# Decoder step on one core: k's projections issued before q's, part of each mLSTM head's preparation issued during q's projections, and 23 warm-up matmuls for 11

## The chip, the cores and the metric

One Trainium2 chip, one of its cores. The metric is the device time of one execution in microseconds (us); a single core runs the whole program.

## The reference, cut to what matters

One layer of a decoder for 1024 prompt tokens and 32 sample tokens (8 sequences of 4), width 1024. Each token is normalised and multiplied by `w_in`; the columns give the gMLP branch (u, v), the mLSTM branch (q, k, v, o and two gates per head) and two merge gates.

```python
qk = silu(causal_conv(qk_pad, conv_w, conv_b, T))      # q and k: 4-tap convolution over time
q, k = heads(qk[..., :W]), heads(qk[..., W:]) * 256 ** -0.5     # 4 heads of 256
...
# per head and chunk of tokens, C, n, m carried along:
s   = exp(dmat - m_t) * einsum('td,sd->ts', q, k)      # dmat: masked log decays
num = w_inter * einsum('vd,td->tv', C, q) + einsum('ts,sv->tv', s, v)
C   = decay * C + einsum('s,sv,sd->vd', w_in, v, k)
```

The rest (spatial gating, the two projections, `w_out`, a SwiGLU FFN and the norms) is the same in both kernels and is not touched by the change.

## The kernel before, in words

Every product in f32 is split: an operand becomes a rounded part (hi, fp32r) and a remainder (lo), and three matmuls stand for one. The input is kept transposed in `hT` (8 pairs of hi and lo, 128 x 1056).

A projection of 128 columns is one `TJob`: for each of 8 k-steps, 9 matmuls of 352 columns (hi and lo of the input for three column chunks, then the weight's remainder), then `evac`. `prep` of the next job splits its weight tile before the job at hand is run: ScalarE rounds `raw` to `wh` (L154) and VectorE subtracts for `wl` (L155). `wh` and `wl` have two buffers each, and the accumulator `acc` has two. Weights come by DMA on SP's queue into three `raw` buffers.

The order before is, for each head h: two TJobs for q, two for k, then a `Start` that puts the generator `mlstm(h)` into the queue `fill`, then 3 to 6 TJobs for the merge gates, two for o, and for later heads an `AJob` for v. After each k-step of a TJob `tick()` advances the first generator in `fill` to its next `yield`; so the mLSTM work of a head is spread through the projections that follow its k. A k-step is 9 matmuls.

`conv_evac` (q and k) copies `acc` out on ScalarE (L428 to L438), adds three taps on VectorE (L440, L442), applies Silu on ScalarE (L446), and writes the last raw rows through SP (L448).

`mlstm(h, q, k, so)` begins with the decay rows: `E` and `wb`, two of the 34 slots of the pool `S`, are filled by four DMAs from `nm_d` and `wi_d` (L578, L580), which `gates()` wrote in the first two projections of head 0. VectorE adds the mask to `E` (L588, L589), and ScalarE takes nine exponentials (L591, L592). After four more ticks comes `s1(0)`: 32 small transposes of k for token chunks 0 to 3 (`kt_part(0, n)`, L605), 8 of the 32 for chunks 4 to 7 (`kt_part(1, 0)`), the scores' two matmuls into the bank `s_ps`, `E = s_ps * E` on VectorE (L628), the scaled k (`kw`, L632, L633) and the split v (`vsp`). `s1(1)` to `s1(3)` have 8 transposes each. `s2(j)` has the state update's matmuls into two banks `u_ps`, `s3(j)` the output's into `n_ps`. The loop is

```python
        for _ in range(4):
            yield
        s1(0)
        yield
        for j in range(8):
            if j < 7:
                s1(j + 1)
                yield
            sq = s2(j)
            yield
            s3(j, *sq)
            yield
```

`s_ps`, `u_ps`, `n_ps` and other small results share the PSUM pool `pm` with two buffers; a new one waits until an older one was read. Except for the first stretch, where ScalarE, VectorE and SP have the written order, the Tile scheduler sets each engine's order; each engine then executes its own queue in that order.

At the start, 11 matmuls of zeros (`NWARM`, tile `wz`) run before the first data are there, and then `VStart`: for each 128 tokens the products of `hT` with two heads' v columns (`acc_v`), which need `avh` and `avl` (L206, L207) and the split input `hh`, `hl` (L382, L383).

Of the kernel before, what the change touches and what calls it, by code (L numbers as in the profile page):

```python
# [9 lines left out]
F32 = mybir.dt.float32  # L10
# [4 lines left out]
P = 128  # L15
D = 1024
TP = 1024
TS = 32
T = TP + TS
KT = D // P  # L20
H = 4
DH = 256
# [4 lines left out]
NF = DFF // P  # L27
EPS = 1e-6
NEG = -3.0e38
NWARM = 11  # L30
NCST = 4
FCH = ((0, 512), (512, 256), (768, 288))
REDO = (6, 7)
# [6 lines left out]
def hybrid_step_kernel(  # L40
# [9 lines left out]
    PE, V, A, G, SP = nc.tensor, nc.vector, nc.scalar, nc.gpsimd, nc.sync  # L50
# [4 lines left out]
    mp = ctx.enter_context(tc.tile_pool(name="mp", bufs=2))  # L55
# [4 lines left out]
    def S(name, dt=F32):  # L60
        return sp.tile([P, SLOT_W], dt, tag="s", name=name)

    def bank(name):
        return pm.tile([P, 512], F32, tag="sm", name=name)

    def f(ap):
        return ap.bitcast(F32)
# [48 lines left out]
    def mm(out, l, r, start, stop):  # L116
        PE.matmul(out, l, r, start=start, stop=stop)  # L117
# [160 lines left out]
    def add(job):  # L278
        jobs.append(job)
        for i, (src, j) in enumerate(job.parts):  # L280
            parts.append((src, job, i))
        job_end.append(len(parts))
# [30 lines left out]
    hT = [(S(f"hh{k}", F32R), S(f"hl{k}", F32R)) for k in range(KT)]  # L313
# [87 lines left out]
    vtiles = {}  # L401
# [17 lines left out]
    def conv_evac(kind, h, dt, dst):  # L419
        ct = 8 * kind + 2 * h + dt  # L420

        def ev(acc):
            raw = S("raw_qk")
            rs = raw[:, 1027:1083].rearrange("p (b s) -> p b s", s=7)
            G.memset(raw[:, 0:3], 0.0)
            G.tensor_copy(rs[:, :, 0:3],
                          scT[:, 24 * ct:24 * (ct + 1)].rearrange("p (b r) -> p b r", r=3))
            A.activation(raw[:, 3:707].rearrange("p (a c) -> p a c", c=CW), acc[:, 0:2, :CW], AF.Copy)  # L428
            A.activation(raw[:, 707:1027], acc[:, 2, 0:320], AF.Copy)
            A.activation(rs[:, :, 3:7], acc[:, 2, 320:352].rearrange("p (b t) -> p b t", t=LT), AF.Copy)  # L430
            c = S("qk")
            cs = c[:, TP:T].rearrange("p (b t) -> p b t", t=LT)

            def w(j):
                return cvw[:, 16 * j + ct:16 * j + ct + 1]
            A.activation(c[:, 0:704].rearrange("p (a c) -> p a c", c=CW), acc[:, 0:2, :CW], AF.Identity,
                         scale=w(3), bias=w(4))
            A.activation(c[:, 704:T], acc[:, 2, :CW], AF.Identity, scale=w(3), bias=w(4))  # L438
            for j in range(3):
                V.scalar_tensor_tensor(c[:, :TP], raw[:, j:j + TP], w(j), c[:, :TP],  # L440
                                       op0=ALU.mult, op1=ALU.add)
                V.scalar_tensor_tensor(cs, rs[:, :, j:j + 4], w(j), cs, op0=ALU.mult, op1=ALU.add)  # L442
            co = mp.tile([P, 27], F32, tag="co", name="co")
            G.tensor_copy(co[:, 0:3], raw[:, 1024:1027])
            G.tensor_copy(co[:, 3:27].rearrange("p (b r) -> p b r", r=3), rs[:, :, 4:7])
            A.activation(c[:, :T], c[:, :T], AF.Silu)  # L446
            dst[dt] = c
            SP.dma_start(conv_out[ct], co)  # L448
        return ev
# [118 lines left out]
    def colv(i, j, h, n=P):  # L568
        return cols[:n, i, 4 * j + h:4 * j + h + 1]

    def mlstm(h, q, k, so):
        E, wb = S("E"), S("wb")
        vs = vtiles.pop(h)

        def vt(j):
            return vs[j // 3][:, j % 3]
        for dst, src in ((E, nm_d), (wb, wi_d)):
            SP.dma_start(dst[:, :TP].rearrange("p (j t) -> p j t", t=P),  # L578
                         src[0:32].rearrange("(j h) t -> h j t", h=H)[h:h + 1].to_broadcast([P, 8, P]))
            SP.dma_start(dst[:, TP:T], src[32 + h:33 + h, 0:TS].to_broadcast([P, TS]))  # L580
        cst = {}

        def load_c(b):
            c = mp.tile([P, 2, DH], F32, tag="cst", bufs=NCST, name="cst")
            SP.dma_start(c, state_C[0, b, h].rearrange("(v p) d -> p v d", p=P))
            cst[b] = c
        E3 = E[:, :TP].rearrange("p (j t) -> p j t", t=P)
        V.tensor_tensor(E3, E3, maskneg.unsqueeze(1).to_broadcast([P, 8, P]), op=ALU.add)  # L588
        V.tensor_tensor(E[:TS, TP:T], E[:TS, TP:T], masks_s, op=ALU.add)  # L589
# [1 line left out]
            A.activation(E3[:, j], E3[:, j], AF.Exp, bias=colv(0, j, h))  # L591
        A.activation(E[:TS, TP:T], E[:TS, TP:T], AF.Exp, bias=colv(0, 8, h, TS))  # L592
        yield
        qk = {}
        Cx = [None, None, None]

        kts, vsp = {}, []

        def kt_part(g, n):
            if n == 0:  # L600
                kts[g] = S("kt")[:, :D].rearrange("p (j a c) -> p j a c", a=2, c=P)
            for i in range(8 * n, 8 * n + 8):
                dt, a, b = i // 16, i // 4 % 4, i % 4
                x = k[dt][32 * a:32 * a + 32, 512 * g:512 * (g + 1)].rearrange("p (j t) -> p j t", t=P)
                V.transpose(out=kts[g][32 * b:32 * b + 32, :, dt, 32 * a:32 * a + 32],  # L605
                            in_=x[:, :, 32 * b:32 * b + 32])

        def split(hi, lo, x, eng=V):
            A.activation(hi, x, AF.Copy)
# [7 lines left out]
        def s1(j):  # L617
            js = slice(P * j, P * (j + 1))
            if j == 0:
                for n in range(4):  # L620
                    kt_part(0, n)
            if j < 4:
                kt_part(1, j)
            b = bank("s_ps")
            for dt in range(2):
                mm(b[:, 0:P], k[dt][:, js], q[dt][:, js], dt == 0, dt == 1)
            sT = mp.tile([P, 2, P], F32R, tag="sT", name="sT")
            V.scalar_tensor_tensor(E3[:, j], b[:, 0:P], 0.0625, E3[:, j], op0=ALU.mult, op1=ALU.mult)  # L628
            split(sT[:, 0], sT[:, 1], E3[:, j])
            kt = kts[j // 4][:, j % 4].rearrange("p a c -> p (a c)")  # L630
            kw = mp.tile([P, 2, DH], F32R, tag="cst", bufs=NCST, name="kw")
            A.activation(kw[:, 0], kt, AF.Copy, scale=colv(1, j, h))  # L632
            V.scalar_tensor_tensor(kw[:, 1], kt, colv(1, j, h), f(kw[:, 0]), op0=ALU.mult, op1=ALU.subtract)  # L633
            if j == 0:
                vsp.append(S("vsp", F32R)[:, :1032].rearrange("p (b i n) -> p b i n", b=2, n=258))
            v2 = [vsp[0][:, j % 2, i] for i in range(2)]
            split(*v2, vt(j)[:, 0:258])
            qw = None
            if j > 0:
                qw = mp.tile([P, 2, 2 * P], F32R, tag="cst", bufs=NCST, name="qw")  # L640
                for dt in range(2):
                    G.tensor_tensor(q[dt][:, js], q[dt][:, js], wb[:, js], op=ALU.mult)
                    split(*(qw[:, i, P * dt:P * (dt + 1)] for i in range(2)), q[dt][:, js], G)
            qk[j] = (sT, kw, qw, v2)
# [29 lines left out]
                A.activation(Cx[2][:, 0], Cx[0], AF.Copy)  # L674
                V.tensor_tensor(Cx[2][:, 1], Cx[0], f(Cx[2][:, 0]), op=ALU.subtract)

        for _ in range(4):
            yield
        s1(0)
        yield  # L680
        for j in range(8):
            if j < 7:
# [12 lines left out]
        b = bank("st_ps")  # L695
# [30 lines left out]
        b = bank("ss_ps")  # L726
# [15 lines left out]
        for bb in range(NB):  # L742
# [4 lines left out]
            c = cst.pop(bb)  # L747
# [6 lines left out]
            b = bank("cu_ps")  # L754
# [11 lines left out]
        b = bank("sn_ps")  # L766
# [22 lines left out]
        for j in range(9):  # L789
            n = P if j < 8 else TS  # L790
# [8 lines left out]
        for j in range(9):  # L799
            n = P if j < 8 else TS  # L800
# [3 lines left out]
        for dt in range(2):  # L804
            for g in range(3):
                b = bank("hT_ps")
                js = range(4 * g, min(4 * g + 4, 9))
                w = 0
                for j in js:
                    n = P if j < 8 else TS  # L810
# [312 lines left out]
    def wcol(c, k):  # L1123
        return w_in[COL[c] + k]
# [7 lines left out]
    qs = [dict() for _ in range(H)]  # L1132
    ks = [dict() for _ in range(H)]
# [4 lines left out]
    class Start(Job):  # L1138
# [3 lines left out]
        def run(self):  # L1142
            self.fn()

    for h in range(H):
        for dt in range(2):
            add(TJob(wcol("q", 2 * h + dt), KT, hT, conv_evac(0, h, dt, qs[h])))
        for dt in range(2):
            add(TJob(wcol("k", 2 * h + dt), KT, hT, conv_evac(1, h, dt, ks[h])))
        add(Start(lambda h=h: fill.append(mlstm(h, qs[h], ks[h], sos[h]))))  # L1150
        for _ in range((6, 3, 3, 4)[h]):
            i, k = glist[gi]
            gi += 1
            add(TJob(wcol("ga" if i == 0 else "gb", k), KT, hT, sig_evac(i, k)))
        for dt in range(2):
            add(TJob(wcol("o", 2 * h + dt), KT, hT, o_evac(sos[h], dt)))
        if h + 1 < H:
            if h:
                add(AJob(COL["v"] + 2 * (h + 1), hT, v_evac(h + 1)))
        else:  # L1160
            while gi < 16:
                i, k = glist[gi]
                gi += 1
                add(TJob(wcol("ga" if i == 0 else "gb", k), KT, hT, sig_evac(i, k)))
# [6 lines left out]
    for k in range(KT):  # L1171
        j = TJob(wcol("u", k), KT, hT, u_evac(k))
# [9 lines left out]
    for k in range(KT):  # L1182
# [6 lines left out]
        j = TJob(w_proj_b[k], KT, b_op, pb_evac(k))  # L1189
# [5 lines left out]
    for k in range(KT):  # L1195
# [8 lines left out]
        j = TJob(w_proj_a[k], KT, a_op, pa_evac(k))  # L1204
# [3 lines left out]
    for k in range(KT):  # L1208
# [4 lines left out]
        j = TJob(w_out[k], KT, m_op, wo_evac(k))  # L1213
# [52 lines left out]
    wps = bank("warm_ps")  # L1266
    for _ in range(NWARM):
        mm(wps, wz[:, :P], wz, True, True)
# [132 lines left out]
```

## Time and profile before

| | us |
|---|---|
| median of 3 runs | 1988.68 |
| the three runs | 1987.43, 1988.68, 1989.14 |
| profiled execution: span from first to last instruction | 1987.8 |
| what the median has beyond that span | 0.9 |
| TensorE busy in it | 1946.1 (98%) |
| VectorE busy in it | 968.7 (49%) |
| ScalarE busy in it | 554.4 (28%) |

For the profiled execution only its span is given as a time of its own; it lies inside the range of the three runs. In the views PE is TensorE, PEld its weight loads, DVE VectorE, ACT ScalarE, POOL GpSimd and SPq the queue from which SyncE issues DMAs. Lines L... are those of the kernel's source. A bracket at the end of a timeline row tells how long the engine was idle before it and what ended the wait. PEclk is the granted share of TensorE's clock: 1.00 is 2.4 GHz, 0.50 is 1.2 GHz.

### The profile page before, as it was taken

How to read it: one execution, taken by the hardware profiler on the slowest of the kernel's cores; microseconds unless marked ns; L12 is line 12 of the kernel's file. 1: busy time of each engine (PE TensorE's matmuls, PEld its weight loads, DVE VectorE, ACT ScalarE, POOL GpSimd, SP SyncE). 2: the span in 40 equal slices, each digit the busy share in tenths (PEclk: the TensorE clock that was granted, in tenths of full speed). 3: DMA queues.
4: the chain of work that ended last, by engine and by line, in shares of the span. 5: the costliest groups of instructions: out<-in, count | busy, mean ns of one | idle time of the engine just before them, and what ended most of it. 6: DMA issues, size and time to landing. Idle time of an engine off the chain costs nothing.

```text
span 1987.8 us, 30709 instructions
## 1 busy us (share of the span) xinstructions
PE 1946.1 (98%) x12673; PEld 1917.1 (96%) x12673; DVE 968.7 (49%) x2199; ACT 554.4 (28%) x945; POOL 259.7 (13%) x315
## 2 busy tenths in 40 slices
PE   8989998998998999999999999999999999999998
PEld 7989998998998999999999999999999999999997
DVE  7776758768677683614323214232323232333235
ACT  6544245235324422213211114211111111111123
POOL 0102102101210210011002311101010010101012
PEclk9999999999999999999999999999999999999999
DMA  6223531622522343124743321020211111110212
GB/s 231 69 77 121 185 88 51 212 85 68 168 96 87 121 164 104 30 85 171 259 156 130 118 87 54 23 73 24 63 34 53 40 46 51 35 59 27 75 43 88
DMA packets 81112, 186.43 MB, mean 94 GB/s; under 512 B 11355, under 2 KB 43756, under 8 KB 80972
## 3 DMA queue, kind: packets, MB, share of 16 engines
q1 hardware_dynamic: 80540, 184.18, 28.1%
q8 instruction: 99, 1.62, 0.3%
q14 instruction: 41, 0.34, 0.1%
q10 hardware_dynamic: 432, 0.30, 0.1%
HBM read 148.49 MB, written 35.95 MB: 93 GB/s over the span
## 4 chain that ended last, share of the span: by engine, by line
PE 88%; DVE 8%; DMA 1%; ACT 1%; issue 1%; SPq 0%; POOL 0%; DVEq 0%; ACTq 0%; POOLq 0%
PE acc L117 71%; PE acc_a L117 7%; DVE kt L605 4%; PE fin_ps L117 2%; PE n_ps L117 1%; PE acc_v L117 1%; PE u_ps L117 1%; PE acc_f L117 1%; PE sp_ps L117 1%; DVE qk L440 1%; DVE junk L751 1%; PE hT_ps L122 0%; DMA qb<-qs_d 0%; PE s_ps L117 0%; PE cu_ps L117 0%
## 5 line engine op out<-in xcount | busy, mean ns | idle before, releaser
L117 PE MATMUL acc<-hh,wh 128*128 128x352 f32 x1152 | 379.0, 331 | 0.0
L117 PE MATMUL acc<-hl,wh 128*128 128x352 f32 x1152 | 373.6, 326 | 0.0
L154 ACT ACTIVATE wh<-raw 128x1024 fp32r<-128x1024 f32 (+1 forms) x164 | 148.1, 903 | 790.9 <-PE acc L117 785.4
L117 PE MATMUL acc<-h2h,wh 128*128 128x352 f32 x1056 | 338.8, 323 | 0.0
L117 PE MATMUL acc<-h2l,wh 128*128 128x352 f32 x1056 | 338.6, 322 | 0.0
L117 PE MATMUL acc<-hh,wl 128*128 128x352 f32 x1152 | 252.2, 326 | 0.0
L117 PE MATMUL acc<-h2h,wl 128*128 128x352 f32 x1056 | 226.5, 322 | 0.0
L117 PEld LDWEIGHTS acc<-hh,wh 128*128 128x128 f32 x1152 | 218.8, 190 | 2.2 <-PE ss_ps L117 1.6
L117 PEld LDWEIGHTS acc<-hl,wh 128*128 128x128 f32 x1152 | 219.9, 191 | 0.2
L155 DVE TENSOR_TENSOR wl<-raw,wh 128x1024 fp32r<-128x1024 f32 (+1 forms) x164 | 167.5, 1021 | 102.5 <-ACT wh L154 102.4
L117 PEld LDWEIGHTS acc<-h2l,wh 128*128 128x128 f32 x1056 | 199.8, 189 | 0.1
L117 PEld LDWEIGHTS acc<-h2h,wh 128*128 128x128 f32 x1056 | 198.2, 188 | 0.0
L117 PEld LDWEIGHTS acc<-hh,wl 128*128 128x128 f32 x1152 | 197.4, 190 | 0.1
L117 PEld LDWEIGHTS acc<-h2h,wl 128*128 128x128 f32 x1056 | 178.8, 188 | 0.0
L1022 POOL TENSOR_TENSOR tu<-tu,tg 128x1056 f32<-128x1056 f32 x22 | 68.0, 3091 | 646.6 <-DVE tu L1021 646.6
L117 PE MATMUL acc<-ah,wh 128*128 128x352 f32 x432 | 138.6, 323 | 0.0
L117 PE MATMUL acc<-al,wh 128*128 128x352 f32 x432 | 138.5, 322 | 0.0
L117 PE MATMUL acc<-or,wh 128*128 128x352 f32 x384 | 123.4, 323 | 0.5 <-DVE or L914 0.4
L1021 DVE TENSOR_TENSOR tu<-acc,rB 128x1056 f32<-128x1056 f32 x22 | 27.7, 1257 | 196.1 <-PE acc L117 196.1
L117 PE MATMUL acc<-oh,wh 128*128 128x352 f32 x384 | 123.2, 323 | 0.0
L117 PE MATMUL acc_a<-avh,hh 128*128 128x256 f32 (+1 forms) x432 | 121.0, 284 | 0.1
L751 DVE CUSTOM_DVE_ANT_0 junk<-cst,qb 128x256 f32<-128x256 f32 x256 | 111.2, 435 | 20.1 <-DMA qb<-qs_d 11.1
(347 smaller groups left out, 3389.8 us busy)
## 6 DMA issues: line engine op xcount, KB each, us to landing
raw<-in_w_in_dram SPq DMA_DIRECT2D x62, 512.0 KB
raw<-in_w_ffn_in_dram SPq DMA_DIRECT2D x44, 512.0 KB
qb<-qs_d SPq DMA_DIRECT2D x32, 512.0 KB
raw<-in_w_ffn_out_dram SPq DMA_DIRECT2D x48, 192.0 KB
sig_d<-sig SPq DMA_DIRECT2D x16, 528.0 KB
sigl<-sig_d SPq DMA_DIRECT2D x16, 528.0 KB
cst<-in_state_C_dram SPq DMA_DIRECT2D x32, 256.0 KB
out_C_sample_dram<-cst SPq DMA_DIRECT2D x32, 256.0 KB
```

The lines of the kernel that those rows point to most:

```text
L117: PE.matmul(out, l, r, start=start, stop=stop)
L154: A.activation(self.wh[:, :kt], raw[:, :kt], AF.Copy)
L155: V.tensor_tensor(self.wl[:, :kt], raw[:, :kt], f(self.wh[:, :kt]), op=ALU.subtract)
L440: V.scalar_tensor_tensor(c[:, :TP], raw[:, j:j + TP], w(j), c[:, :TP], op0=ALU.mult, op1=ALU.add)
L605: V.transpose(out=kts[g][32 * b:32 * b + 32, :, dt, 32 * a:32 * a + 32], in_=x[:, :, 32 * b:32 * b + 32])
L751: V.tensor_tensor_reduce(junk, c[:, v], qq[:, DH * t:DH * (t + 1)], 1.0, 0.0, ALU.mult, ALU.add, numI[:, v, LT * bb + t:LT * bb + t + 1])
L1021: V.tensor_tensor(a3(tu), acc[:, :, :CW], a3(rB["r"]), op=ALU.mult)
L1022: G.tensor_tensor(tu[:, :T], tu[:, :T], tg[:, :T], op=ALU.mult)
```

## The change

A head's k is projected before its q. The beginning of `mlstm` becomes a generator of its own, `mlstm_lead`, which the two q TJobs advance by one step at each k-step, from their `hook`: first the four DMAs for `E` and `wb`, then 16 of the 32 transposes for chunks 0 to 3 in six steps, then the mask and the nine exponentials, then the other 16 in six steps. The 32 transposes for chunks 4 to 7 stay in `s1(0)` to `s1(3)`. `mlstm` waits five ticks rather than one and four, and has one more `yield` after `s1(0)`. `NWARM` goes from 11 to 23.

```diff
-NWARM = 11
+NWARM = 23
-    def mlstm(h, q, k, so):
-        E, wb = S("E"), S("wb")
...
+    lead = {}
+
+    def kt_block(kt, k, g, i):
+        dt, a, b = i // 16, i // 4 % 4, i % 4
+        x = k[dt][32 * a:32 * a + 32, 512 * g:512 * (g + 1)].rearrange("p (j t) -> p j t", t=P)
+        V.transpose(out=kt[32 * b:32 * b + 32, :, dt, 32 * a:32 * a + 32],
+                    in_=x[:, :, 32 * b:32 * b + 32])
+
+    def mlstm_lead(h, k):
+        E, wb, kt = S("E"), S("wb"), new_kt()
+        lead[h] = (E, wb, kt)
         for dst, src in ((E, nm_d), (wb, wi_d)):
             SP.dma_start(dst[:, :TP].rearrange("p (j t) -> p j t", t=P),
...
+        yield
+        for n in range(6):
+            for i in range(16 * n // 6, 16 * (n + 1) // 6):
+                kt_block(kt, k, 0, i)
+            yield
         E3 = E[:, :TP].rearrange("p (j t) -> p j t", t=P)
         V.tensor_tensor(E3, E3, maskneg.unsqueeze(1).to_broadcast([P, 8, P]), op=ALU.add)
...
         A.activation(E[:TS, TP:T], E[:TS, TP:T], AF.Exp, bias=colv(0, 8, h, TS))
         yield
+        for n in range(6):
+            for i in range(16 + 16 * n // 6, 16 + 16 * (n + 1) // 6):
+                kt_block(kt, k, 0, i)
+            yield
+
+    def mlstm(h, q, k, so):
+        E, wb, kt0 = lead.pop(h)
...
         def s1(j):
             js = slice(P * j, P * (j + 1))
             if j == 0:
-                for n in range(4):
-                    kt_part(0, n)
+                kts[1] = new_kt()
             if j < 4:
-                kt_part(1, j)
+                for i in range(8 * j, 8 * j + 8):
+                    kt_block(kts[1], k, 1, i)
...
-        for _ in range(4):
+        for _ in range(5):
             yield
         s1(0)
+        yield
         yield
...
+    def lead_hook(h):
+        def hook(_):
+            if h not in leads:
+                leads[h] = mlstm_lead(h, ks[h])
+            next(leads[h], None)
+        return hook
+
     for h in range(H):
         for dt in range(2):
-            add(TJob(wcol("q", 2 * h + dt), KT, hT, conv_evac(0, h, dt, qs[h])))
+            add(TJob(wcol("k", 2 * h + dt), KT, hT, conv_evac(1, h, dt, ks[h])))
         for dt in range(2):
-            add(TJob(wcol("k", 2 * h + dt), KT, hT, conv_evac(1, h, dt, ks[h])))
+            j = TJob(wcol("q", 2 * h + dt), KT, hT, conv_evac(0, h, dt, qs[h]))
+            j.hook = lead_hook(h)
+            add(j)
         add(Start(lambda h=h: fill.append(mlstm(h, qs[h], ks[h], sos[h]))))
```

## Rows read from the trace of the kernel before

**Rows 1.** The page's first part: busy time of each engine, its share of the span, its instructions.

```profile
PE 1946.1 (98%) x12673; PEld 1917.1 (96%) x12673; DVE 968.7 (49%) x2199; ACT 554.4 (28%) x945; POOL 259.7 (13%) x315
```

**Rows 2.** What TensorE waited for over the whole span: us in total, times, the longest.

```profile
PE u_ps L117 <- DVE E L628: 22.3, 10, 5.0
...
PE cu_ps L117 <- DVE cst L759: 1.9, 1, 1.9
```

**Rows 3.** TensorE's timeline at the scores and the first state update: start, us, and what it waited for. The first four are of head 0, then one each of heads 1, 2 and 3, then one of head 0's next chunks.

```profile
124.99 0.61 PE L117 MATMUL s_ps<-qk 128*128 128x128 f32 x4
126.89 0.61 PE L117 MATMUL s_ps<-qk 128*128 128x128 f32 x4
132.62 0.48 PE L117 MATMUL acc<-hh,wl 128*128 128x352 f32 x2
138.09 0.55 PE L117 MATMUL u_ps<-vsp,kw 128*128 128x258 f32 x1 [4.98 <-DVE E L628]
...
309.82 0.55 PE L117 MATMUL u_ps<-vsp,kw 128*128 128x258 f32 x1 [4.99 <-DVE E L628]
...
472.50 0.55 PE L117 MATMUL u_ps<-vsp,kw 128*128 128x258 f32 x1 [4.99 <-DVE E L628]
...
634.38 0.55 PE L117 MATMUL u_ps<-vsp,kw 128*128 128x258 f32 x1 [4.99 <-DVE E L628]
...
152.49 0.63 PE L117 MATMUL u_ps<-vsp,kw 128*128 128x258 f32 x3 [0.48 <-DVE E L628]
```

**Rows 4.** VectorE's timeline of head 0, from the end of its second k projection.

```profile
117.16 1.23 DVE L155 TENSOR_TENSOR wl<-raw,wh 128x1024 fp32r<-128x1024 f32 x1 [4.87 <-ACT wh L154]
119.65 1.28 DVE L440 SCALAR_TENSOR_TENSOR qk<-raw_qk,vall,qk 128x1024 f32<-128x1024 f32 x1 [1.26 <-ACT qk L438]
...
123.73 1.22 DVE L588 TENSOR_TENSOR E<-E,maskneg 128x1024 f32<-128x1024 f32 x1
...
124.97 12.65 DVE L605 STREAM_TRANSPOSE kt<-qk 32x128 f32<-32x128 f32 x40
137.65 0.29 DVE L628 SCALAR_TENSOR_TENSOR E<-s_ps,E 128x128 f32<-128x128 f32 x1
...
138.70 2.53 DVE L605 STREAM_TRANSPOSE kt<-qk 32x128 f32<-32x128 f32 x8
```

**Rows 5.** Busy time of each engine in the stretch from (about) the start of each head's u_ps row to where the clock is back at full: PE, PEld, DVE, ACT and POOL busy (instructions), granted clock, DMA share, GB/s. Heads 0 to 3.

```profile
138.09:141.06 2.97, 2.97 (x11) 2.97 (x12) 2.84 (x10) 1.69 (x3) 0.00 (x0) 0.50 0.39 152
...
309.98:315.14 5.16, 5.16 (x20) 5.16 (x20) 4.62 (x16) 1.83 (x4) 0.00 (x0) 0.50 0.26 105
...
472.60:475.57 2.97, 2.97 (x11) 2.97 (x12) 2.84 (x10) 1.59 (x3) 0.00 (x0) 0.50 0.39 161
...
634.50:639.41 4.91, 4.91 (x18) 4.91 (x19) 4.66 (x16) 1.88 (x4) 0.00 (x0) 0.50 0.30 115
```

**Rows 6.** The same columns for the last two of a head's four projections (23.2 us for two), heads 0 and 2, for one undisturbed projection of head 2, for the one before it, and for 11 us of head 0's chunks.

```profile
92.90:116.10 23.20, 23.20 (x147) 23.20 (x146) 10.69 (x14) 10.63 (x17) 0.88 (x6) 1.00 0.29 72
...
427.30:450.50 23.20, 23.20 (x147) 22.63 (x147) 14.02 (x24) 8.00 (x12) 0.99 (x6) 1.00 0.43 116
...
438.95:450.47 11.52, 11.52 (x74) 11.52 (x73) 5.39 (x7) 4.57 (x7) 0.36 (x2) 1.00 0.57 152
...
424.86:438.95 14.09, 14.09 (x92) 13.38 (x91) 11.06 (x24) 5.85 (x8) 0.98 (x4) 1.00 0.24 67
...
138.95:150.00 11.05, 10.81 (x67) 10.52 (x67) 10.75 (x33) 4.54 (x12) 2.29 (x4) 0.90 0.28 99
```

**Rows 7.** ScalarE's timeline: the Silu of head 0's k in the projection before the last, then that of its last one with what follows it.

```profile
112.39 1.09 ACT L446 ACTIVATE qk<-qk 128x1056 f32<-128x1056 f32 x1 [4.36 <-DVE qk L442]
...
123.91 1.09 ACT L446 ACTIVATE qk<-qk 128x1056 f32<-128x1056 f32 x1 [4.36 <-DVE qk L442]
125.01 1.28 ACT L591 ACT_TABLE_LOAD   x1
126.31 2.46 ACT L591 ACTIVATE E<-E,cols 128x128 f32<-128x128 f32 x8
```

**Rows 8.** Head 2: VectorE's weight remainder for its last projection, and SP's queue from which the weights and the decay rows come.

```profile
434.50 1.22 DVE L155 TENSOR_TENSOR wl<-raw,wh 128x1024 fp32r<-128x1024 f32 x1
...
435.78 0.34 SPq L289 DMA_DIRECT2D raw<-in_w_in_dram  x1
...
453.44 0.41 SPq L289 DMA_DIRECT2D raw<-in_w_in_dram  x1
453.90 0.42 SPq L580 DMA_DIRECT2D E<-nm_d  x1
```

**Rows 9.** The start: the warm-up matmuls, the first matmuls of v on either side of the change from 1.2 to 2.4 GHz, TensorE's next wait, the last VectorE operation that the second v product needs, and the granted clock in the first stretch of v.

```profile
1.35 4.10 PE L117 MATMUL warm_ps<-wz 128*128 128x512 bf16 x11 [1.35 <-DVE wz L1265]
8.11 0.58 PE L117 MATMUL acc_v<-avh,hh 128*128 128x256 f32 x1 [2.66 <-ACT avh L206]
...
14.33 0.42 PE L117 MATMUL acc_v<-avh,hh 128*128 128x264 f32 x1
...
29.50 0.49 PE L117 MATMUL rb_ps<-idn,rw 128*128 128x128 f32 x2 [1.42 <-DVE rw L375]
...
14.08 0.19 DVE L218 TENSOR_TENSOR avl<-graw,avh 128x32 fp32r<-128x32 f32 x1
...
8.11:14.77 6.66, 6.52 (x28) 6.22 (x29) 6.32 (x17) 6.09 (x16) 0.00 (x0) 0.50 1.03 416
```

More of the change, by code (lines that the diff above doesn't have):

```diff
@@ L569, in colv, with new_kt @@
         return cols[:n, i, 4 * j + h:4 * j + h + 1]
-    def mlstm(h, q, k, so):
-        E, wb = S("E"), S("wb")
-        vs = vtiles.pop(h)
-        def vt(j):
-            return vs[j // 3][:, j % 3]
+    lead = {}
[4 more added lines that the diff above has]
+                    in_=x[:, :, 32 * b:32 * b + 32])
+    def new_kt():
+        return S("kt")[:, :D].rearrange("p (j a c) -> p j a c", a=2, c=P)
+    def mlstm_lead(h, k):
+        E, wb, kt = S("E"), S("wb"), new_kt()
+        lead[h] = (E, wb, kt)
         for dst, src in ((E, nm_d), (wb, wi_d)):
@@ L580, in mlstm @@
             SP.dma_start(dst[:, TP:T], src[32 + h:33 + h, 0:TS].to_broadcast([P, TS]))
[L581 to L586, printed above, removed]
+        yield
[3 more added lines that the diff above has]
+            yield
         E3 = E[:, :TP].rearrange("p (j t) -> p j t", t=P)
@@ L593, in mlstm, with vt, load_c @@
         yield
+        for n in range(6):
[4 more added lines that the diff above has]
+        E, wb, kt0 = lead.pop(h)
+        E3 = E[:, :TP].rearrange("p (j t) -> p j t", t=P)
+        vs = vtiles.pop(h)
+        def vt(j):
+            return vs[j // 3][:, j % 3]
+        cst = {}
+        def load_c(b):
+            c = mp.tile([P, 2, DH], F32, tag="cst", bufs=NCST, name="cst")
+            SP.dma_start(c, state_C[0, b, h].rearrange("(v p) d -> p v d", p=P))
+            cst[b] = c
         qk = {}
         Cx = [None, None, None]
[L597 to L606, printed above, removed]
+        kts, vsp = {0: kt0}, []
         def split(hi, lo, x, eng=V):
@@ L1143, in run @@
             self.fn()
+    leads = {}
+    def lead_hook(h):
[4 more added lines that the diff above has]
+        return hook
     for h in range(H):
         for dt in range(2):
-            add(TJob(wcol("q", 2 * h + dt), KT, hT, conv_evac(0, h, dt, qs[h])))
+            add(TJob(wcol("k", 2 * h + dt), KT, hT, conv_evac(1, h, dt, ks[h])))
         for dt in range(2):
-            add(TJob(wcol("k", 2 * h + dt), KT, hT, conv_evac(1, h, dt, ks[h])))
+            j = TJob(wcol("q", 2 * h + dt), KT, hT, conv_evac(0, h, dt, qs[h]))
+            j.hook = lead_hook(h)
+            add(j)
         add(Start(lambda h=h: fill.append(mlstm(h, qs[h], ks[h], sos[h]))))
```

## The prediction

> **What bounds the kernel now.** I read the page's first part first: TensorE is busy 1946.1 of 1987.8 us, VectorE half the span [rows 1]. So the kernel is TensorE's program, and a change can only win where TensorE stands still or runs slowly. The view of waits tells where it stands: 22.3 us, in 10 waits of at most 5.0, are the state update `u_ps` waiting for VectorE's L628; the other waits I look at are 1.9 and 2.66 us [rows 2, 9]. The timeline then shows four waits of 4.98 to 4.99 us, one a head, just at the first `u_ps` of a head [rows 3]: 19.95 us of the 22.3.
>
> What is late there is read from VectorE's queue in head 0. After the last projection's convolution it adds the mask, and then runs 40 transposes in one block, 12.65 us (0.316 each); only behind them comes L628, at 137.65 [rows 4]. Its input, the scores, was made at 124.99 [rows 3]. L628 is the reader that frees a bank of `pm`: the two `s_ps` held both, so `u_ps` could not begin before one was read. TensorE ran projection matmuls until 133.1 and then had nothing left ahead of `u_ps` in its queue.
>
> Each wait has a second price. Behind it the granted clock is 0.50 (1.2 GHz) for 2.97, 5.16, 2.97 and 4.91 us, with TensorE busy throughout [rows 5]. At 2.4 GHz the same matmuls take half, so this is 16.01 / 2 = 8.0 us. The two prices together, 28.0 us or 1.4%, are what the main part of the change can reach.
>
> **The change part by part.**
>
> *The 32 transposes for chunks 0 to 3* are moved from behind the convolution of the second pair of projections to beside the matmuls of that pair: 32 x 0.316 = 10.1 us of VectorE a head. With k first, k's Silu is done well before q's matmuls end, so the inputs are there. Is there room? In that pair's 23.2 us VectorE is busy 10.69 us in head 0 [rows 6]; with the transposes and the mask (1.22 + 0.17, about 1.4 [rows 4]) it is 22.2 of 23.2: full, but not over. In head 2 the previous head's last work is still in it, 14.02 us, and the sum is 25.5: 2.3 us too many. Behind the last projection VectorE has about that much slack before the convolution's taps can start: it is idle 1.26 us before L440 and `wl` can move [rows 4]. I take 0.5 us of delay a head at the first scores, between nothing (the idle 4.87 us before 117.16 used as well) and 2.5.
>
> *What is left before L628* are the 8 transposes of `s1(0)` for chunks 4 to 7: 8 x 0.316 = 2.53 us [rows 4]. Scores at 124.99 in head 0's time, VectorE free at about 123.7 (the mask has gone ahead), so L628 comes at about 126.5 and not 137.65. `u_ps` stands a tick later than written before, two for the first scores to `u_ps`: three k-steps of about 1.5 us behind 124.99, 129.4. The bank is free 3 us before. The wait of 4.98 us goes, and with it, since the engine no longer stands still for 5 us, the stretch at 1.2 GHz: minus 28.0 us in four heads.
>
> *The extra `yield`* moves `s1(1)` and all behind it by one k-step of the next projection. It adds no instruction; TensorE has projection matmuls in between, nothing to nothing.
>
> *The mask and exponentials* come earlier. ScalarE: a table load of 1.28, eight exponentials 2.46 [rows 7] and a small one 0.31. Before, Silu, Exp and Sigmoid follow each other, one load each; now Exp lies between k's Silu and q's, so that Silu's table is loaded once more: 4 x 1.28 = 5.1 us of ScalarE. It is busy 10.63 of 23.2 us in those projections [rows 6], 16 with all this: hidden. If it delayed the evacuation of `acc`, there is a second `acc` and a whole projection, 11.52 us [rows 6], of cover.
>
> *The four DMAs* for `E` and `wb` go out two projections earlier, ahead of two weight loads on SP's queue; one issue takes about 0.42 [rows 8], four some 1.8 us. A weight is issued more than a projection before it is used. What waits for them is the mask on VectorE, and behind it in the queue the transposes of the second half of k, the next `wl` and q's taps. The three slots that are held two projections longer (`E`, `wb`, `kt`) are there: in head 0, where most are held, I count in the code 16 for the input, 6 for v, 4 for q and k, 2 for raw rows and these 3, 31 of 34. I take nothing; the other bound is a late weight, priced as rival B.
>
> *23 warm-up matmuls.* Eleven take 4.10 us, and the first v matmul starts 2.66 us later, at 8.11, because `avh` is late; it and the next 27 run at a granted 0.50 until 14.77 [rows 9]. Twelve more at 0.21 to 0.43 us (4.10 us hold both: 512 columns are 0.21 at 2.4 GHz, 0.43 at 1.2) end between 8.0 and 10.6. If the clock stays at 2.4 GHz, the 28 take half. But the second v product needs L218, which ends at 14.27, and began at 14.33 [rows 9]; and at 28 us TensorE waits 1.42 us for x's own chain anyway. So at most 0.4 us are won, and I think none is left after 29.50: 0, between minus 0.4 and plus 2.5 (the end at 10.6 with nothing made up). The Trainium skill ("TensorE: Matmul & The Clock Gate", Part 1) says that the array is throttled by default and activity releases the throttle; by that alone the gain would be half of 6.66 us, 3.3, and the sum 1959.4. The rows of ScalarE and VectorE speak against it, since the operands would not be there.
>
> *What stays:* small waits of `u_ps` of 0.24 to 0.7 us, 22.3 - 19.95 = 2.3 in all, as [rows 3] shows one at 152.49. In the 11 us from 138.95 VectorE is busy 10.75 [rows 6], working off its backlog. Without the backlog they could vanish; but `s1(1)` to `s1(3)` keep 2.53 us of transposes each. I leave them as they are.
>
> Sum, against the profiled span: 1987.8 - 28.0 + 4 x 0.5 = 1961.8 us. The median of the runs is 0.9 above that span, so 1962.7 us.
>
> **The rivals.**
>
> *A, a new wait takes part of it back.* The scores and `u_ps` still share two banks, and VectorE is now nearly full in q's projections. If the 8 transposes of `s1(0)` stand whole before L628 while VectorE is 2.3 us late (head 2's sum), `u_ps` or `s_ps` waits 2.5 us a head, 10 in all, and half the heads keep a slow stretch of 4: 10 + 2 x 2 = 14, or 1988.7 - 28 + 14 = 1974.7. For it: 22 to 25 us of VectorE work in 23.2. Against: its slack behind the last projection. The Trainium skill ("Perfetto Trace Analysis", Identifying Performance Opportunities) says that a gap that repeats on the engine that should be full can mean too few buffers, PSUM included. By that rule two banks and not the transposes would be the fault, and part of the wait would stay, as here.
>
> *B, slower: VectorE is blocked before a weight's remainder.* VectorE works in the order of its queue. If the mask stands ahead of `wl` and waits for decay rows, which on SP stand behind a weight load that waits for a buffer (in head 2 one left at 435.78, and `E`'s second DMA waited until 453.90 behind another [rows 8]), the next projection starts late. `wl` has little slack there: 434.50 + 1.22 against 438.95, 3.2 us [rows 6, 8]. It costs the idle time and up to 2.5 us at 1.2 GHz. To eat 28 us it needs 7 a head, so it decides from 4.5 us of idle. With 8 idle it is 4 x 10.5 = 42, or 2002.7. Against: before, the mask never waited; VectorE had no gap in front of it.
>
> *C, the change does not do what it says.* The scheduler sets the order, and it may leave the transposes late. For it: before, k's first half was ready at 113.5 [rows 7], VectorE then stood idle until 117.16 [rows 4], and still no transpose was there. Against: they now stand a whole projection earlier in the program, and with them the mask. It would give 1988.7.
>
> *D, better:* the small waits go too (2.3), the delay is nothing (2.0), and head 3's wait of `cu_ps` (1.9 [rows 2]) falls away: 1956.5.
>
> **How the numbers follow.** The forecast 0.58, D 0.06, A 0.25, C 0.05, B 0.06. The forecast's own range is 1957 to 1969 (the bounds of the delay, 0 to 2.5 a head, with the warm-up's). To leave out no more than 2 in 10 the range reaches into A, to 1977, and down to 1956. What the three runs spread over is 0.09%; 0.2%, 4 us, is what I count as a difference. Faster: 0.58 + 0.06 + 0.25 = 0.89; the same 0.05; slower 0.06.
>
> **What would show it.** Right: no wait of 5 us at `u_ps`, its total under 5 us; no stretch at 0.50 between 76 and 680 us; VectorE's busy time the same (nothing is removed) but with 8 transposes in a block rather than 40; VectorE over 20 of 23.2 us in q's projections; ScalarE with four more table loads. The warm-up right: v's first matmuls at 2.4 GHz, and the matmul after the wait for `rw` within 0.5 us of 29.5. Wrong by A: waits of 2 us at `s_ps` or `u_ps`, some still followed by 0.50. Wrong by B: `acc` waiting for `wl` L155. Wrong by C: L605 still in blocks behind q's taps. Another kind of error: the head's gain given back where VectorE's sample work of head 3 ends, between 680 and 745 us.

## The result and the profile after

| | before | after |
|---|---|---|
| median of 4 runs, us | 1988.23 | 1970.59 (1968.83 to 1972.2) |
| profiled execution: span, us | 1987.8 | 1967.0 (its own time 1968.83) |

The ratio is 0.9908, 95% interval 0.9894 to 0.9922: 0.9% faster, 17.6 us. The forecast was 1962.7, so 26 us of gain were expected and two thirds came. A second set of runs of the same kernel gave 0.9909 (below); its profiled span was 1970.9, so what is read term by term from one execution can be off by some 4 us.

The page's first part and what TensorE waited for, answering to [rows 1, 2]:

```profile
PE 1939.5 (99%) x12685; PEld 1909.8 (97%) x12685; DVE 974.3 (50%) x2199; ACT 560.9 (29%) x949; POOL 258.3 (13%) x315
...
PE s_ps L117 <- ACT qk L446: 5.2, 4, 2.0
PE u_ps L117 <- DVE E L644: 4.1, 3, 1.4
PE rb_ps L117 <- DVE rw L375: 2.1, 2, 1.8
...
PE cu_ps L117 <- POOL km L763: 1.3, 1, 1.3
```

The four 5 us waits at `u_ps` are gone: 22.3 us have become 4.1, three waits of 1.35 or 1.36 us at a later chunk. In their place stands a wait that was not there: at `s_ps`, TensorE waits for the Silu of q, once a head, 5.2 us in all. TensorE's timeline of head 0 shows where, against [rows 3]:

```profile
124.61 0.39 PE L117 MATMUL s_ps<-qk 128*128 128x128 f32 x2
...
128.92 0.49 PE L117 MATMUL s_ps<-qk 128*128 128x128 f32 x2 [2.00 <-ACT qk L446]
...
130.21 0.92 PE L117 MATMUL s_ps<-qk 128*128 128x128 f32 x4
...
133.57 0.97 PE L117 MATMUL u_ps<-vsp,kw 128*128 128x258 f32 x6
```

The first scores no longer come in one piece. The matmuls with q's first half run at 124.61; those with the second half, 4.3 us later, behind 12 projection matmuls and 2.00 us of idle. `u_ps` then has no wait. The reason is in ScalarE's timeline of that stretch:

```profile
106.16 0.95 ACT L436 ACTIVATE qk<-acc,vall 128x704 f32<-128x704 f32 x1
107.12 1.28 ACT L598 ACT_TABLE_LOAD   x1
108.42 2.45 ACT L598 ACTIVATE E<-E,cols 128x128 f32<-128x128 f32 x8
...
110.99 0.62 ACT L438 ACTIVATE qk<-acc,vall 128x352 f32<-128x352 f32 x1
...
118.62 1.28 ACT L446 ACT_TABLE_LOAD   x1 [1.82 <-DVE qk L442]
119.92 1.09 ACT L446 ACTIVATE qk<-qk 128x1056 f32<-128x1056 f32 x1
120.91 0.74 ACT L428 ACTIVATE raw_qk<-acc 128x704 f32<-128x704 f32 x1
```

q's second projection ended at about 116.1, and its evacuation (L428) began only at 120.91. It stood behind the Silu of q's first half, and that Silu waited for VectorE's taps (114.38), which VectorE's timeline has behind two blocks of 16 transposes. The first row, taps of k's second half, is the end of a long idle stretch of VectorE:

```profile
96.63 1.28 DVE L440 SCALAR_TENSOR_TENSOR qk<-raw_qk,vall,qk 128x1024 f32<-128x1024 f32 x1 [4.89 <-ACT qk L438]
...
101.85 5.04 DVE L576 STREAM_TRANSPOSE kt<-qk 32x128 f32<-32x128 f32 x16
106.92 1.22 DVE L595 TENSOR_TENSOR E<-E,maskneg 128x1024 f32<-128x1024 f32 x1
...
109.31 5.04 DVE L576 STREAM_TRANSPOSE kt<-qk 32x128 f32<-32x128 f32 x16
114.38 1.28 DVE L440 SCALAR_TENSOR_TENSOR qk<-raw_qk,vall,qk 128x1024 f32<-128x1024 f32 x1
...
120.39 2.50 DVE L576 STREAM_TRANSPOSE kt<-qk 32x128 f32<-32x128 f32 x8
123.52 1.29 DVE L440 SCALAR_TENSOR_TENSOR qk<-raw_qk,vall,qk 128x1024 f32<-128x1024 f32 x1 [0.63 <-ACT qk L438]
```

The last taps before began at 119.65 [rows 4], now at 123.52, 3.9 us later. This is the whole delay of the scores in head 0: from L428's start to the scores' last input the distance is 8.0 us in head 0 of both kernels (before, L428 at 117.03 and scores at 124.99; after, 120.91 and 128.92), and also in the other heads of the changed one (287.5 and 295.51, 445.06 and 453.07, 602.62 and 610.63). The scores come late by as much as the evacuation does.

Windows of the changed kernel, columns as in [rows 5, 6]: q's two projections of heads 0 and 2, two stretches of TensorE at half clock (behind the 2.00 us wait; and in the start, behind the 1.8 us wait of `rb_ps`), and the start from the warm-up matmuls on, now at full clock:

```profile
92.93:115.97 23.04, 23.04 (x147) 23.04 (x145) 18.87 (x45) 14.19 (x28) 1.03 (x8) 1.00 0.30 96
...
417.50:440.60 23.10, 23.10 (x147) 22.56 (x146) 22.51 (x54) 11.52 (x22) 2.65 (x7) 1.00 0.37 118
...
130.35:133.76 3.41, 3.41 (x15) 3.41 (x14) 3.31 (x9) 2.46 (x6) 1.92 (x4) 0.50 0.02 5
31.36:34.78 3.42, 3.42 (x19) 3.42 (x18) 2.99 (x16) 3.09 (x13) 0.00 (x0) 0.50 0.06 24
...
4.06:14.77 10.71, 8.67 (x48) 5.48 (x46) 8.29 (x21) 8.39 (x22) 0.06 (x2) 1.00 1.01 384
```

The four stretches of [rows 5] are one of 3.41 us. The first scores of heads 1, 2 and 3 come 4.3, 9.9 and 14.2 us earlier than before, the last `n_ps` of head 3 18.0 (663.0 for 681.0), the end of the sample work behind head 3 20.1, the end of the program 20.8: each head gives about 4 to 6 us where 6.5 were expected, and nothing is given back later.

### The profile page after: what moved, and what is told of

It is laid out like the page before. It is cut to its first block, busy times and chain, and to the rows that moved or that the text cites. A ratio compares the mean times of both kernels' runs of the same rounds, so it can differ in the third digit from the quotient of the medians.

```text
span 1967.0 us, 30743 instructions
## 1 busy us (share of the span) xinstructions
PE 1939.5 (99%) x12685; PEld 1909.8 (97%) x12685; DVE 974.3 (50%) x2199; ACT 560.9 (29%) x949; POOL 258.3 (13%) x315
## 4 chain that ended last, share of the span: by engine, by line
PE 63%; DVE 0%; ACT 0%; issue 0%; DVEq 0%; ACTq 0%
PE acc L117 55%; PE acc_a L117 4%; PE fin_ps L117 2%; PE sp_ps L117 1%; PE acc_f L117 1%; PE f_ps L122 0%; DVE y L1135 0%; PE r_ps L117 0%; PE hT_ps L122 0%; ACT y L1133 0%; PE sn_ps L117 0%; ACT L846 0%; DVE cst L776 0%; DVE y L1125 0%; DVEq L1425 0%
## 5 line engine op out<-in xcount | busy, mean ns | idle before, releaser
L117 PE MATMUL acc_a<-avl,hh 128*128 128x256 f32 (+1 forms) x432 | 119.6, 281 | 0.0
```

## The experiments

The first question was which part of the change gives what; the second, why a new wait came.

**Warm-up alone undone.**

```diff
-NWARM = 23
+NWARM = 11
```

> The changed kernel with 11 warm-up matmuls instead of 23. Theory (the start is bound by the operands, not by TensorE's clock): the first v matmuls run at 1.2 GHz again, the wait for rw near 28 us is shorter by as much, and the time stays at the changed kernel's 1970.6 us within 1.5. Rival W (the warm-up is part of the gain): half of the 6.7 us at 1.2 GHz comes back, 1973.9 us.

1972.69 us, ratio 0.9916 (0.9903 to 0.993). That is 2.1 us above 1970.6, outside the 1.5 of the theory and nearer to rival W's 1973.9; but the interval overlaps that of the changed kernel and holds rival W's time too, so the time does not decide. The traces do: the first projection begins at 67.74 with 11 matmuls and at 67.77 with 23 (68.49 in the second set with 23):

```profile
67.77 0.32 PE L117 MATMUL acc<-hh,wh 128*128 128x352 f32 x1
```

```profile
67.74 0.32 PE L117 MATMUL acc<-hh,wh 128*128 128x352 f32 x1
```

With 11, v's first matmuls take 0.58 us and then 0.41 again, as at 1.2 GHz before, though this profile's record of the granted clock shows no fall there; with 23 they take 0.38 and 0.28. The second v product begins at 14.20 with 11 and at 14.11 with 23. So nothing of the clock's gain is left at the first projection. The waits at `s_ps` and `u_ps` in the heads are the same: the 12 matmuls cannot be told from nothing.

**The order alone** (k first and 23 warm-ups; decay rows, mask, exponentials and all 32 transposes back behind q).

```diff
     def mlstm(h, q, k, so):
+        E, wb = S("E"), S("wb")
...
-                kts[1] = new_kt()
+                kts[0], kts[1] = new_kt(), new_kt()
+                for i in range(32):
+                    kt_block(kts[0], k, 0, i)
```

> k before q and 23 warm-up matmuls, but the decay rows, the mask, the exponentials and all 32 transposes are back at the beginning of the head's mLSTM, behind q's projections. Theory (the wait at the first u_ps comes from the block of 40 transposes in front of L628): the four waits of 5 us and the slow stretches behind them are all back, 1988 us within 2. Rival O (it is the order of q and k that gives the gain, because the last taps are then on q and the transposes' input is older): the block can start earlier by the 5.3 us of wl and taps, waits under 1 us, about 1970 us.

1989.08, ratio 0.9999 (0.9989 to 1.0008); the waits at `u_ps` are back:

```profile
PE u_ps L117 <- DVE E L637: 21.9, 9, 5.0
```

Projecting k first gives nothing by itself; it lets k's transposes be issued beside q's projections.

**Only the transposes early; only the rows, mask and exponentials early.** In the first, the four DMAs, mask and exponentials go to the head of `mlstm`; in the second, the two loops over `kt_block` leave `mlstm_lead` for `s1(0)`.

```diff
     def mlstm_lead(h, k):
-        E, wb, kt = S("E"), S("wb"), new_kt()
+        kt = new_kt()                            # first kernel
+        E, wb = S("E"), S("wb")                  # second kernel
```

> The 32 transposes stay in q's projections, but decay rows, mask and exponentials are back at the beginning of the head's mLSTM. Theory (transposes are the cause; the exponentials in ScalarE's queue ahead of q's evacuation cost part of the gain, the 5.2 us that TensorE waits at s_ps for q's Silu): s_ps waits fall to under 2 us in all, no new wait since the exponentials still end before u_ps, 1964 to 1968 us. Rival R (the rows moved early are needed too, since L628 reads E): u_ps waits 2 us or more a head for E, with slow stretches behind it, 1978 us or more.

> Only the decay rows, mask and exponentials are issued during q's projections; the 32 transposes are back in s1(0), in one block with the 8 for the other chunks. Theory: the block of 12.7 us still stands in front of L628 and only the mask's 1.4 us in front of it are gone, so the waits at u_ps are 3.6 us a head, and half of the slow stretches stay: 1980 to 1986 us. Rival R (the rows were the cause): waits under 1 us a head, about 1970 us.

Transposes only: 1976.72, ratio 0.9933 (0.9921 to 0.9945), 9 us above the top of what was expected. Rows only: 1985.36, 0.998 (0.9971 to 0.9989), as expected. Their waits, the first kernel's above:

```profile
PE u_ps L117 <- DVE E L644: 10.2, 8, 1.4
PE n_ps L117 <- DVE Cx L671: 3.5, 4, 0.9
PE s_ps L117 <- ACT qk L446: 2.9, 3, 1.3
```

```profile
PE u_ps L117 <- DVE E L640: 16.5, 6, 4.1
```

So in us against before: order 0, rows 4, transposes 13, both 18. The parts add to within 1 us. With the transposes only, the mask and more transposes stand behind q's taps: between VectorE's first two readings of scores there are 9 transposes, not 4, and `u_ps` waits more. `s_ps` waits less, 2.9 us, for the last evacuation starts at 118.10 in head 0 and not at 120.91, and the scores follow it by 8.0 us again (126.11). So the early rows have a price at `s_ps`, smaller than what they save at `u_ps`.

**Where in q's projections the early work stands.** Mask and exponentials ahead of all transposes:

```diff
-        for n in range(6):
-            for i in range(16 * n // 6, 16 * (n + 1) // 6):
-                kt_block(kt, k, 0, i)
+        for _ in range(2):
             yield
...
         yield
+        for n in range(6):
+            for i in range(16 * n // 6, 16 * (n + 1) // 6):
+                kt_block(kt, k, 0, i)
+            yield
```

> The changed kernel with mask and exponentials issued four steps earlier in the lead, ahead of all its transposes. Theory V (the waits left at s_ps come from the order: the exponentials stood ahead of the first q evacuation on ScalarE, its Silu came late, and the second q evacuation queued behind that Silu): s_ps waits fall from 5.2 to under 2 us, 1966 to 1968 us. Rival T (VectorE's total work in q's projections is what makes q late, in whatever order): s_ps waits stay at 4 to 6 us, 1970 to 1972 us.

1981.52, ratio 0.996 (0.9948 to 0.9973): worse than either theory. VectorE's timeline:

```profile
105.03 10.11 DVE L576 STREAM_TRANSPOSE kt<-qk 32x128 f32<-32x128 f32 x32
115.17 1.28 DVE L440 SCALAR_TENSOR_TENSOR qk<-raw_qk,vall,qk 128x1024 f32<-128x1024 f32 x1
...
119.25 1.22 DVE L155 TENSOR_TENSOR wl<-raw,wh 128x1024 fp32r<-128x1024 f32 x1
```

The scheduler puts all 32 transposes in one block as soon as they are ready, ahead of q's taps and of the next weight's remainder. `acc` now waits for `wl` (4.8 us, longest 3.6), `s_ps` 8.5 us.

**The early work one projection earlier**, and the same with 16 of the second 32 transposes added at q's end (the hook also on k's second projection, five more steps ahead of the blocks, which come in four steps of 4; in the second kernel `s1(0)` to `s1(3)` keep 4 transposes each).

```diff
-            add(TJob(wcol("k", 2 * h + dt), KT, hT, conv_evac(1, h, dt, ks[h])))
+            j = TJob(wcol("k", 2 * h + dt), KT, hT, conv_evac(1, h, dt, ks[h]))
+            if dt:
+                j.hook = lead_hook(h)
+            add(j)
```

> The lead begins one projection earlier, in k's second one: transposes of k's first half from its end on, mask and exponentials and the second half's transposes in q's first projection, nothing in q's last six k-steps. Theories V and T both expect the s_ps waits to go (under 1 us); the u_ps waits of 1.4 us in three heads stay, since the 8 transposes in each of s1(0) to s1(3) stay: 1964 to 1967 us. Rival P (two PSUM banks, whatever VectorE does): the wait only moves from s_ps to u_ps, 1970 us or more.

> As the kernel with the earlier lead, and 16 of the 32 transposes for chunks 4 to 7 are issued at the end of q's second projection, so that s1(0) to s1(3) have 4 each instead of 8. Theory V: 4 x 0.316 = 1.3 us less in front of each L628, the u_ps waits fall under 1 us in all and no stretch at 1.2 GHz is left in the heads, 1960 to 1964 us. Rival T (VectorE is full there, so q's second evacuation is late again): s_ps waits come back, 1967 us or more.

1993.25, ratio 1.002 (1.0011 to 1.0029), and 2010.92, 1.0107 (1.0093 to 1.0121): both slower than before. In the first, VectorE stands in its queue for the decay rows' DMA in head 0 (first row), and the weight's remainder behind it is late for TensorE (second). Larger waits come on top: 7.96 us at head 0's first scores (third), where the scheduler put the second score matmul right behind the first, and 9.2 us in heads 2 and 3 at `hT_ps`, the transposed output of the head before (fourth): 13 transposes (4.10 us) stand ahead of VectorE's L824, for which it waits. In the second kernel 24 transposes (fifth) stand ahead of q's last taps, and the first scores wait (sixth):

```profile
102.40 1.23 DVE L600 TENSOR_TENSOR E<-E,maskneg 128x1024 f32<-128x1024 f32 x1 [9.66 <-DMA E<-nm_d]
...
109.61 1.25 PE L117 MATMUL acc<-hh,wl 128*128 128x352 f32 x3 [3.05 <-DVE wl L155]
...
138.75 0.79 PE L117 MATMUL s_ps<-qk 128*128 128x128 f32 x2 [7.96 <-ACT qk L446]
...
433.34 0.30 PE L122 MATMUL hT_ps<-idn,v 128*128 128x128 f32 x1 [4.47 <-DVE v L824]
```

```profile
125.90 7.60 DVE L576 STREAM_TRANSPOSE kt<-qk 32x128 f32<-32x128 f32 x24
...
141.84 0.80 PE L117 MATMUL s_ps<-qk 128*128 128x128 f32 x2 [12.69 <-ACT qk L446]
```

**The changed kernel again**, no edit.

> The changed kernel itself, beside the others on the same chip: 0.9908 of the kernel before, within 0.0015. Its four timed runs lay between 1968.8 and 1972.2 us; the waits at s_ps (5.2 us) and u_ps (4.1 us) should come out the same, and only stretches at 1.2 GHz elsewhere differ.

1971.89, ratio 0.9909 (0.9894 to 0.9925); `s_ps` 5.2, `u_ps` 5.4.

**The order set by hand.** First the exponentials behind ScalarE's evacuation of q's first half and 16 transposes behind its taps; then, beside that, the 8 transposes of each block behind that block's scores.

```diff
+        with tc.issue_after(behind[0, h, 0][0]):
             for j in range(8):
                 A.activation(E3[:, j], E3[:, j], AF.Exp, bias=colv(0, j, h))
...
+                with tc.issue_after(behind[0, h, 0][1]):
+                    for i in range(16 + 16 * n // 6, 16 + 16 * (n + 1) // 6):
+                        kt_block(kt, k, 0, i)
...
+            if j < 4:                            # second kernel
+                with tc.issue_after(lo):
+                    for i in range(8 * j, 8 * j + 8):
+                        kt_block(kts[1], k, 1, i)
```

> The changed kernel with two orders set by hand: the exponentials stand behind ScalarE's evacuation of q's first half, and the second 16 transposes behind the taps of q's first half on VectorE. Nothing is left out. Theory Q (an engine's queue order decides: what stands ahead of q's evacuation and taps delays the first score block): the taps of q's first half start some 5 us earlier than in the changed kernel, the waits at s_ps fall from 5.2 us to under 2 us, and the slow-clock stretch behind head 0's wait goes. But 12 transposes (12 x 0.316 = 3.8 us) now stand between VectorE's reading of the first and of the second score block, so the waits at u_ps grow from 4.1 to 6 to 9 us; the sum is about that of the changed kernel, a ratio to the kernel before of 0.989 to 0.992 (1966 to 1972 us). Rival T (the amount of VectorE's work in q's projections decides, not its order): the waits at s_ps stay at 4 to 6 us and those at u_ps at 4 to 5, with the same ratio of 0.990 to 0.992; the waits, not the time, tell them apart here.

> As the kernel with q first, and the 8 transposes of k's second half that each of the first four blocks issues stand behind that block's score readings on VectorE (its read of the score bank and its remainder). Nothing is left out. Theory Q: the waits at s_ps stay under 2 us, those at u_ps under 3 us, and no stretch at the slow clock is left between 76 us and 680 us but for those of the kernel's other stages; the gain over the changed kernel is 3 + 1 + half of 3.4, about 5 us, a ratio to the kernel before of 0.986 to 0.989 (1960 to 1966 us). Rival T (VectorE's total work decides): the delay moves to another wait (n_ps, or the weights' remainders), and the ratio stays at 0.990 to 0.992 (1969 to 1972 us).

1980.0, ratio 0.9951 (0.9936 to 0.9966), and 1993.76, 1.002 (1.0011 to 1.0029): two misses, with 13.1 and 9.6 us of waits at `s_ps` where under 2 were expected. In the first, q's taps did begin 4.8 us earlier (109.55), yet the evacuation of q's second half hardly did, because `kw` now stood ahead of it on ScalarE and waited for the 16 transposes; and TensorE's second score matmul had no projection work ahead of it any more:

```profile
118.70 0.91 ACT L653 ACTIVATE kw<-kt,cols 128x256 fp32r<-128x256 f32 x2 [2.54 <-DVE kt L579]
...
120.46 0.73 ACT L430 ACTIVATE raw_qk<-acc 128x704 f32<-128x704 f32 x1
...
129.34 0.80 PE L117 MATMUL s_ps<-qk 128*128 128x128 f32 x2 [4.10 <-ACT qk L449]
```

In the second, each 8 transposes (2.5 us) stand between a block's scores and the copy of its state, and `n_ps` waits 18.1 us (9.5 and 8.6). The amount of VectorE's work is the same in both kernels and in the changed one (974.5, 975.5 and 974.3 us busy); what differs is what stands behind what.

**ScalarE's order set** (exponentials behind the evacuation of q's first half, `kw` behind that of its second), and the same with the transposes of the third and fourth block behind the reading of the second and third.

```diff
+            with tc.issue_after(behind[0, h, 1]):
+                A.activation(kw[:, 0], kt, AF.Copy, scale=colv(1, j, h))
...
+                with tc.issue_after(read[j - 1]) if j > 1 else nullcontext():    # second kernel
+                    for i in range(8 * j, 8 * j + 8):
+                        kt_block(kts[1], k, 1, i)
```

> The changed kernel with ScalarE's order alone set by hand: the exponentials stand behind the evacuation of q's first half, and the first parts of kw behind the evacuation of q's second half. Nothing is left out and no VectorE instruction is given a place. Theory S (ScalarE executes in order; in the changed kernel q's second projection ends at 116.1 us, and its evacuation starts only at 120.91, behind a Silu that waits for taps; in the kernel with q first it starts at 120.46, behind kw, which waited 2.5 us for 16 transposes): the evacuation starts within 1.5 us of the projection's end, q's last Silu ends 1 us or more earlier, and the waits at s_ps fall to 2 us or less in all (5.2 in the changed kernel, 13.1 in that with q first). In the order that results, 9 transposes (9 x 0.316 = 2.8 us) stand between VectorE's readings of the first and the second score block, so 4 to 10 us of waits at u_ps remain; ratio to the kernel before 0.987 to 0.992. Rival T (the amount of VectorE's work in q's projections makes the scores late): the waits at s_ps stay at 4 us or more.

> As the kernel with ScalarE's order set, and k's transposes that belong to the third and fourth block stand behind VectorE's reading of the second and third score block. Nothing is left out. Between the readings of the first and second block then stand 2 transposes and not 9. Theory S with a queue on VectorE: s_ps waits of 2 us or less as there, u_ps waits under 3 us, no stretch at the slow clock behind heads 0 to 3, so 5.2 + 4.1 - 5 = 4 us and half of 3.4 us less than the changed kernel: a ratio to the kernel before of 0.986 to 0.9895 (1961 to 1967 us), faster than both kernels. Rival T: the transposes only move the wait to n_ps (18 us of it where all of them stood behind the scores), and the ratio is 0.991 or above.

1976.58, ratio 0.993 (0.9918 to 0.9943), and 1976.61, 0.9931 (0.9917 to 0.9944): faster than before, but not than the changed kernel. The first kernel's ScalarE, VectorE and TensorE:

```profile
117.18 0.74 ACT L430 ACTIVATE raw_qk<-acc 128x704 f32<-128x704 f32 x1
...
120.02 2.19 DVE L578 STREAM_TRANSPOSE kt<-qk 32x128 f32<-32x128 f32 x7
122.24 1.29 DVE L442 SCALAR_TENSOR_TENSOR qk<-raw_qk,vall,qk 128x1024 f32<-128x1024 f32 x1
...
127.64 0.49 PE L117 MATMUL s_ps<-qk 128*128 128x128 f32 x2 [2.23 <-ACT qk L448]
```

The evacuation is 3.7 us earlier than in the changed kernel, as theory S said. Only 1.3 us of it reach the scores: VectorE has 16 transposes, a remainder and 7 more transposes ahead of the last taps, which could have begun behind the evacuation at 119.7. And TensorE waits no less, 8.1 us in all, since the scheduler put the second score matmul right behind the first, where the changed kernel has 12 projection matmuls. The second kernel took the waits at `u_ps` from 6.0 to 2.4 us and got 3.9 at `n_ps` for it. With the transposes only, evacuation and scores of head 0 both come 2.8 us earlier than in the changed kernel (118.10 and 126.11), but there mask and exponentials have moved too; with ScalarE's order alone set, the scores do not follow the evacuation in full. What stays open: a kernel with all three queues set for this stretch was not run.

## Why the prediction was right and where it was off

The sign, the range and the mechanism held: the four waits of 5 us were VectorE's block of 40 transposes, and with it moved they are gone; the rows alone do not remove them, the transposes do. The size was 7.9 us off. Of these 5.2 lie in the span (1967.0 for 1961.8), 0.9 in what a run has beside its span (1.8 in the profiled run, not 0.9), and 1.8 between that run and the median. The span, term by term (3.2 + 1.7 + 1.8 too little in the heads, some 2.3 too much behind head 3, 0.4 at the start: 4.0 of the 5.2; the rest is in waits of tenths that I did not trace). These are terms of one execution, and the gains behind head 3 and at the start did not come again in the second set:

- *Delay at the first scores, 0.5 us a head, 2.0 in all: measured 5.2,* and a slow stretch of 3.41 us behind it in head 0 (1.7 us). This is the step that failed. I looked for the slack on VectorE, and priced ScalarE at nothing, since a second `acc` covers a late evacuation. That cover is for the next projection's bank, and it held: no `acc` waited. But a late evacuation of the last projection goes straight into the scores, 8.0 us behind it in every head. The exponentials, the Silu that waits for taps and the evacuation share one queue, and the head of the queue waited for VectorE.
- *Small waits of `u_ps`, 2.3 left as they are: measured 4.1.* At the third block of heads 1 to 3, L644 stands behind 4 more transposes and the split of v, 1.35 us each. In the second set, without a slow stretch in head 0, all four heads have this wait, 5.4 in all.
- *The clock, minus 8.0:* the stretches of [rows 5] were 16.01 us, one of 3.41 is left in the heads. Behind head 3 the wait of `cu_ps` shrank from 1.9 to 1.3 us and the stretch at 0.50 behind it, 3.4 us before (first row below), is gone: 0.6 and 1.7 us, part of what rival D named. This was luck: in the second set `cu_ps` waits 2.8 us (second row), and with 11 warm-up matmuls 2.2 (third), there with a stretch of 3.41 us at 0.50 behind it.
- *Warm-up, 0: right.* The first projection began 0.4 us earlier (67.77 for 68.15), but 0.3 later in the second set (68.49). v's first matmuls run at 2.4 GHz from 8.03 (they ran at 1.2 [rows 9]) and then wait for their operands. The wait for `rw` ends at 29.93, later than before's 29.50. The rule of the Trainium skill ("TensorE: Matmul & The Clock Gate", Part 1), that activity releases the throttle, holds in the granted clock (1.00 from 4.06 to 14.77, before 0.50 from 8.11); the 3.3 us do not follow from it, as the run with 11 matmuls shows.
- *Three of the four extra costs priced at nothing were nothing:* DMAs, slots and the extra `yield` left no wait behind.

```profile
714.50:717.90 3.40, 3.40 (x18) 3.40 (x17) 3.15 (x13) 1.14 (x1) 1.19 (x1) 0.50 0.67 194
```

```profile
PE cu_ps L117 <- DVE cst L776: 2.8, 3, 2.3
```

```profile
PE cu_ps L117 <- DVE cst L776: 2.2, 1, 2.2
```

The signs: no wait of 5 us, no block of 40, 4 more table loads (949 for 945 ScalarE instructions) came true; `u_ps` under 5 us did in this run (4.1), not in the second set (5.4). "No stretch at 0.50 between 76 and 680 us" did not, nor VectorE "over 20 of 23.2 us" in head 0: 18.87, for VectorE stands idle in the first 3.7 us of that stretch, until k's second half has been copied out (the 4.89 us before 96.63), although the Silu of k's first half is done at 94.1; head 2 has 22.51.

Rival A was half right: a new wait takes part back, 2.0 us or less a head, but at `s_ps` it is a wait for an operand, not for one of two banks. The 4.1 us left at `u_ps` are waits for the reader of a bank. What the Trainium skill ("Perfetto Trace Analysis", Identifying Performance Opportunities) says, that a gap which repeats can mean too few buffers, was not tested here: no kernel has more banks. What is shown is that with the same two banks the waits at `u_ps` fell from 22.3 to 4.1 us. Rival B's mechanism is real (9.66 us in front of the mask) when the rows are fetched a projection earlier; as changed, the mask did not wait. Rival C fell.

## What to carry to other kernels

Before moving work under cover, list each engine's queue in that stretch, the lightly loaded ones too, and ask of every instruction with a result on the path what would stand ahead of it and what that one waits for. A total of busy time under the length of the stretch is not room: here ScalarE, busy 14.2 of 23.0 us, made the last evacuation 4 us late, since the head of its queue waited for VectorE. And where a scheduler sets the order, a place given to one instruction moves others: 32 transposes into one block, `kw` ahead of an evacuation, two score matmuls together. Each time the trace of the new order has to be read for what stands in front then.

## What the runs showed of the hardware that was not expected

The length of a wait did not tell whether the clock would fall. 2.00 us at the first scores of head 0 was followed by 3.41 us at 0.50 in one run of the changed kernel; in its second set 2.02 us at the same place (row below) was followed by none. In the first kernel with ScalarE's order set, 2.23 us in head 0 was followed by one and 2.75 us in head 1 by none; in the second kernel, 2.22 and 2.76 us at the same two places were both followed by one. And before the change waits of 4.98 and 4.99 us were followed by TensorE working at 0.50 for about 3 us in heads 0 and 2 and about 5 us in heads 1 and 3 [rows 5].

```profile
129.66 0.49 PE L117 MATMUL s_ps<-qk 128*128 128x128 f32 x2 [2.02 <-ACT qk L446]
```
